# Head loads of an attention stage moved to SyncE's queue in 32-row pieces, and S5 outputs loaded some blocks before their use

## The chip, the cores and the metric

The kernel runs on one core of one Trainium2 chip. The metric is the device time of one execution in microseconds (us), given as the median of three runs. Each engine (PE = TensorE, DVE = VectorE, ACT = ScalarE, POOL = GpSimd) works through its own queue of instructions in order. SP (SyncE) issues most of the DMAs, also in order; a DMA issued there goes through the hardware queue, one issued by POOL through the software queue.

## What is computed

Two layers of a trunk for 1024 latent and 128 context tokens of width 1024. Layer 0 projects the normed tokens to queries, keys, values and S5 inputs, runs differential attention (four heads) and an S5 state-space mixer beside each other, and joins them in one output projection; layer 1 is a pooling mixer; each is followed by a squared-ReLU MLP. The change concerns the attention and the gelu of the S5 output:

```python
q, k, v, u = split_in(h, mix_w_in)          # 4 heads, q and k as two halves of 64
s = einsum('bqhmd,bkhmd->bhmqk', q, k) * scale
p = softmax(s, axis=-1)
w = p[:, :, 0] - lam * p[:, :, 1]           # the two halves m = 0, 1
o = einsum('bhqk,bkhe->bqhe', w, v)         # latents: 1024 + 256 keys, context: its own 128
y = (ys[0] + ys[1]) + d_skip * u            # S5 output, two directions
g = gelu(y)
out = g * sigmoid(g @ w_glu)
```

## The kernel before

Matrix products are made of three passes over operands split into a high and a low part. One helper records every engine instruction, so all stand under line L86; groups are told apart by their tiles.

**Projections.** Twelve steps (four heads, each queries, keys, values), each in three blocks of 384 tokens in the order 2, 0, 1, so 36 blocks `n`. `qk_block` rotates a block, splits it into high and low (tile `zz`) and stores it to DRAM scratch `qS` or `kS`; `v_block` transposes a block (tiles `vz`, `pvt`) and stores it to `vS`. `zz`, `vz` and the cached keys `chl` share three buffers (`rp`), so a block's DVE work can have to wait for the store of an earlier one. All engines follow program order in this stage. The scratch is read back by head, since the score product wants 128 rows of (high, low) by 64 channels where the projection wrote blocks of tokens.

**Head loads.** At `n = 31` the tiles of the heads are opened and the unused halves of four `Kl` tiles are zeroed on POOL. From there `load_head(0)` runs one step per block. For each half m it fills `Q` (128 rows of 1152 floats: the high and low part of the queries), `Kd` (128 rows of 1408: the high keys, twice) and 64 rows of `Kl` (the low keys). One head is 3.34 MB. Its nine DMAs were issued by POOL; the values `Vv` come through SP. Heads 1 to 3 are loaded from block 3 of the head before on, one step per block. There are two buffers of each tile.

**Attention.** 36 blocks (4 heads x 9), then two more turns to empty the pipeline. Block i makes its scores (PE, tiles `SP0`, `SP1`), their maximum (DVE, `nm`), the exponentials (ACT, `e`), the combination (ACT and POOL), the transposes and the product with the values (PE). Only PE keeps program order here; the other engines' queues are ordered by the framework's scheduler when the kernel is built. From block 2 on each block also takes one step of `side_work`: the gelu of four S5 channel tiles (`s5_gelu`: `uf` and `yf` loaded, one buffer each; `yf` = `uf` times the skip factor plus `yf` on DVE; square on ACT; two on POOL; tanh on ACT; product on DVE; split on ACT and DVE), and then the split of the `w_glu` weights (tiles `g`).

**After it** come the output projection, the pooling mixer and the two MLPs, from about 760 us to the end.

**SP's semaphores.** SP's DMAs take eight completion counters in turn, so a DMA waits until the one eight before it has landed.

Of the kernel before, what the change touches and what calls it, by code (L numbers as in the profile page):

```python
# [8 lines left out]
F32 = mybir.dt.float32  # L9
# [63 lines left out]
def build(nc, tc, a, o, probe=None):  # L73
    pinned = set()

    class Engine:
# [5 lines left out]
        def __getattr__(self, op):  # L82
            f = getattr(self.e, op)

            def call(*args, **kw):
                ins = f(*args, **kw)  # L86
                if self.name in pinned:
# [5 lines left out]
    V, A, T, P, S_ = (Engine(n, e) for n, e in (("V", nc.vector), ("A", nc.scalar), ("T", nc.tensor),  # L93
                                                ("P", nc.gpsimd), ("S", nc.sync)))
    dma = S_.dma_start
# [24 lines left out]
    def tt(e, out, x, y, op):  # L120
        return e.tensor_tensor(out, x, y, op=op)

    def stt(e, out, x, s, y, op0, op1):
        e.scalar_tensor_tensor(out, x, s, y, op0=op0, op1=op1)
# [4 lines left out]
    qS = dr([HEADS, 2, 2, 2, 32, NTOK], F32, "qS")  # L129
    kS = dr([HEADS, 2, 2, 2, 32, KEYS + TX], F32, "kS")  # L130
# [746 lines left out]
    def load_head(h):  # L877

        Q = [HB([128, NTOK], F32R, f"Q{m}", bufs=2) for m in range(2)]
        Kd = [HB([128, KEYS + TX], F32R, f"Kd{m}", bufs=2) for m in range(2)]  # L880
        Kl = KL[h % 2]
        Vv = HB([128, 11, 128], F32, "Vv", bufs=2)
        l1 = HB([128, 9], F32, "l1", bufs=2)
        hd[h] = (Q, Kd, Kl, Vv, l1)
        cast = P.dma_start
        cast(Q[0], qS[h, :, :, 0])
        for half in range(2):
            cast(Kd[0][64 * half:64 * half + 64], kS[h, 0, :, 0])
        yield
        cast(Kl[0][0:64], kS[h, 1, :, 0])  # L890
        cast(Q[1][0:64], qS[h, 1, :, 1])
        yield
        cast(Q[1][64:128], qS[h, 0, :, 1])
        cast(Kd[1][0:64], kS[h, 0, :, 1])
        yield
        cast(Kd[1][64:128], kS[h, 0, :, 1])
        cast(Kl[1][64:128], kS[h, 1, :, 1])
        yield
        dma(Vv[:, 0:8], vS[h][:, 0:8])
        dma(Vv[:, 10:11], vS[h][:, 10:11])  # L900
        dma(Vv[:, 8:10], a["cache_v"][h].rearrange("p (t e) -> p t e", t=2))
# [55 lines left out]
    for i in range(12):  # L957
        h, kind = divmod(i, 3)
# [4 lines left out]
        for b in (2, 0, 1):  # L963
            p, last, *c = project(w, b)
            cf = c[0] if c else cf
            before(n)
            if n in KN:
                keys_in(KN[n])
            (qk_block if kind < 2 else v_block)(h, *((kind,) if kind < 2 else ()), b, p, cf, lambda: after(n))
            post(n)  # L970
            if b == 2:
                proj_split(i + 1)
            if n == NS + 9:
                S3.close()
                R.close()
                UR.close()
                HB = Pool("heads", side="right")
                KL = [[HB([128, KEYS + TX], F32R, f"Kl{j}{m}") for m in range(2)] for j in range(2)]
                for kl in KL:
                    for m in range(2):  # L980
                        P.memset(kl[m].bitcast(F32)[64 - 64 * m:128 - 64 * m], 0.0)
                loads = load_head(0)
            if loads:
                next(loads, None)
            n += 1
# [152 lines left out]
    def s5_gelu(i):  # L1138

        uf = AT([128, C8, UC], F32, "uf")  # L1140
        yf = AT([128, C8, UC], F32, "yf")
        dma(uf, uS[128 * i:128 * i + 128])
        for g in range(8):
            dma(yf[16 * g:16 * g + 16], yS[8 * i + g].rearrange("(t x) c -> x t c", t=C8))
        yield
        stt(V, yf, uf, dskip[:, i:i + 1], yf, ALU.mult, ALU.add)
        yield
        A.activation(uf, yf, AF.Square)
        yield
        P.tensor_scalar(uf, uf, 0.044715, 1.0, op0=ALU.mult, op1=ALU.add)  # L1150
        tt(P, uf, uf, yf, ALU.mult)
        yield
        A.activation(uf, uf, AF.Tanh, scale=math.sqrt(2.0 / math.pi))
        yield
        stt(V, uf, uf, 1.0, yf, ALU.add, ALU.mult)
        yield
        segs = []
        for u0, u1, b, c0 in ((0, 48, 0, 0), (48, 96, 1, 0), (96, 128, 2, 0), (CX0, UC, 2, 256)):
            c1 = c0 + 8 * (u1 - u0)
            segs.append((uf[:, :, u0:u1], ga[b][:, i, c0:c1].rearrange("p (c s) -> p s c", s=C8),  # L1160
                         ga[b][:, 4 + i, c0:c1].rearrange("p (c s) -> p s c", s=C8)))
        for u, hv, lv in segs:
            A.activation(hv, u, AF.Copy, scale=0.5)
        yield
        for u, hv, lv in segs:
            stt(V, lv, u, 0.5, hv, ALU.mult, ALU.subtract)

    def side_work():

        for i in range(4):  # L1170
            yield from s5_gelu(i)
        yield
        for j in range(4):
            raw = W([128, 4, 128], F32, "raw", bufs=2)
            dma(raw, a["w_glu"][j])
            if j == 1:
                g1 = W([128, 2, 4, 128], F32R, "g1", tag="raw1")
                hi, lo = g1[:, 0], g1[:, 1]
            else:
                hi, lo = (AT([128, 4, 128], F32R, f"g{j}{q}") for q in (1, 2))  # L1180
            A.activation(hi, raw, AF.Copy)
            tt(V, lo, raw, hi, ALU.subtract)
            wgl.append((hi, lo))
            yield
# [12 lines left out]
    for i, t in enumerate(turns):  # L1197
# [3 lines left out]
        if i < nw:  # L1201
            h, qb = work[i]
# [31 lines left out]
        if i < nw:  # L1234
            if qb == 3 and h + 1 < HEADS:
                loads = load_head(h + 1)
            if loads:
                next(loads, None)
# [72 lines left out]
    x, ah = [], []  # L1311
    blk2 = lambda: (BA([128, KT, BX], F32R, "blk", bufs=3), BB([128, KT, BX], F32R, "blk", bufs=3))
    for b in range(NB):
        t = BB([128, KT, BX], F32R, "blk", bufs=3)
        for k in range(4):
            src = hid([128, BN], F32, ("ph", "pl")[k % 2])
# [415 lines left out]
```

## Time and profile before

| | us |
|---|---|
| median of three runs | 2637.35 (2632.61 to 2638.91) |
| the profiled execution | 2634.18 |
| its span | 2632.4 |
| last projection matmul of PE starts at | 415.23 |
| first score matmul of block 1 starts at | 466.05 |
| attention ends about | 733 |

The page gives busy time and share of the span for each engine. A line of the timeline gives the start, the duration, the engine, the operation with out<-in, and in brackets how long the engine had been idle and who released it. The table of windows gives each engine's busy time in a stretch. The list of DMA issues gives the median time from issue to landing.

### The profile page before, as it was taken

To read this page: it belongs to the slowest core of one execution; us is meant where nothing else is said; L and a number is where in the kernel's file an instruction comes from. 1 tells how busy PE (TensorE), PEld (TensorE's weight loads), DVE (VectorE), ACT (ScalarE), POOL (GpSimd) and SP (SyncE) were. 2 spreads that over 40 slices of the span, in tenths; PEclk is the share of its full clock that TensorE was granted. 3 is DMA by queue.
4 is the path that set the end of the run, shared out by engine and by line. 5 is a ranking of instruction groups with operands and counts; after the bars stand their busy time and mean duration, and the time that the engine had idled before them with its cause. 6 is when DMAs were issued, how large, how long until landed. Compare 5 with 4: busy or idle time off the path is not lost.

```text
span 2632.4 us, 36768 instructions
## 1 busy us (share of the span) xinstructions
PE 2457.9 (93%) x14262; PEld 2299.3 (87%) x14262; DVE 1760.9 (67%) x3530; ACT 909.1 (35%) x1679; POOL 381.0 (14%) x346
## 2 busy tenths in 40 slices
PE   7978893786899999999999999999999999999998
PEld 3866693675799799999999999878999999999996
DVE  7489872797869677777767655756555555565554
ACT  4453372776742522222222221554222222122214
POOL 5465513564400000000000000020000000000002
PEclk8988897898999999999999999999999999999999
DMA  6334689445045122232323111011111111111102
GB/s 236 86 107 122 201 205 162 100 88 70 13 160 192 57 89 80 81 96 65 96 73 96 61 41 33 1 41 49 33 49 49 33 49 41 41 41 41 49 9 72
DMA packets 121662, 210.96 MB, mean 80 GB/s; under 512 B 25744, under 2 KB 82832, under 8 KB 121104
## 3 DMA queue, kind: packets, MB, share of 16 engines
q1 hardware_dynamic: 100240, 189.64, 24.2%
q0 software_dynamic: 19008, 13.44, 3.5%
q10 hardware_dynamic: 2240, 5.54, 0.6%
q8 instruction: 113, 1.85, 0.3%
q14 instruction: 61, 0.50, 0.1%
HBM read 176.95 MB, written 31.56 MB: 79 GB/s over the span
## 4 chain that ended last, share of the span: by engine, by line
PE 71%; DVE 8%; DMA 6%; ACT 2%; issue 2%; POOL 1%; SPq 0%; DVEq 0%; ACTq 0%; POOLq 0%
PE p L86 63%; PE nps L86 2%; PE tp L86 2%; PE SP L86 2%; DVE nm L86 1%; DMA yf<-yS 1%; DMA Kl<-kS 1%; DMA raw<-in_w_dram 1%; DVE vv L86 1%; PE pmm L86 1%; DMA raw<-in_mod_v_dram 1%; DMA Kd<-kS 1%; DVE sc L86 1%; DVE mj L86 1%; ACT e L86 1%
## 5 line engine op out<-in xcount | busy, mean ns | idle before, releaser
L86 PE MATMUL p<-blk,wh 128*128 128x384 f32 (+1 forms) x3072 | 794.9, 339 | 0.3 <-DVE r L86 0.3
L86 DVE SCALAR_TENSOR_TENSOR x<-p,modc,x 128x384 f32<-128x384 f32 (+2 forms) x1056 | 513.7, 513 | 165.6 <-PE p L86 160.7
L86 PEld LDWEIGHTS p<-blk,wh 128*128 128x128 f32 x3072 | 559.1, 189 | 13.3 <-issue 11.9
L86 PE MATMUL p<-blk,wl 128*128 128x384 f32 (+1 forms) x1536 | 521.5, 339 | 0.0
L86 PE MATMUL p<-ph,w2h 128*128 128x384 f32 x1536 | 515.1, 335 | 1.8 <-DVE x L86 1.8
L86 PE MATMUL p<-ph,w2l 128*128 128x384 f32 x1536 | 514.4, 335 | 0.0
L86 PE MATMUL p<-pl,w2h 128*128 128x384 f32 x1536 | 513.7, 334 | 0.0
L86 ACT ACTIVATE r<-r,cf 128x384 f32<-128x384 f32 (+2 forms) x256 | 129.9, 531 | 685.8 <-DVE r L86 685.7
L86 PEld LDWEIGHTS p<-ph,w2h 128*128 128x128 f32 x1536 | 288.3, 188 | 7.1 <-DVE x L86 3.7
L86 PEld LDWEIGHTS p<-blk,wl 128*128 128x128 f32 x1536 | 288.8, 188 | 6.5 <-issue 6.2
L86 PEld LDWEIGHTS p<-ph,w2l 128*128 128x128 f32 x1536 | 288.3, 188 | 2.6 <-issue 2.5
L86 PEld LDWEIGHTS p<-pl,w2h 128*128 128x128 f32 x1536 | 288.3, 188 | 0.8 <-issue 0.6
L86 DVE TENSOR_TENSOR r<-p,y 128x384 f32<-128x384 f32 x192 | 106.2, 553 | 207.7 <-PE p L86 194.6
L86 ACT ACTIVATE wh<-raw 128x1024 fp32r<-128x1024 f32 x80 | 84.8, 1060 | 347.4 <-PE p L86 313.6
L86 DVE SCALAR_TENSOR_TENSOR mj<-raw,cb 128x1024 f32<-128x1024 f32 x128 | 156.0, 1219 | 14.4 <-DMA raw<-in_mod_v_dram 13.1
L86 POOL TENSOR_TENSOR pl<-pl,mx 128x256 f32<-128x256 f32 x18 | 14.8, 827 | 1036.8 <-ACT pl L86 1036.8
L86 ACT ACTIVATE w2h<-raw 128x1024 fp32r<-128x1024 f32 x74 | 77.3, 1057 | 222.4 <-PE p L86 173.1
L86 PE MATMUL pmm<-lo,wh 128*128 128x384 f32 (+1 forms) x384 | 138.2, 360 | 6.4 <-DVE lo L86 6.1
L86 PE MATMUL SP<-Kd,Q 128*128 128x512 f32 (+2 forms) x200 | 81.6, 408 | 65.0 <-ACT e L86 28.6
L86 PE MATMUL pmm<-hi,wh 128*128 128x384 f32 (+1 forms) x384 | 141.4, 369 | 0.8 <-ACT wh L86 0.8
L86 PE MATMUL pmm<-hi,wl 128*128 128x384 f32 (+1 forms) x384 | 137.7, 359 | 1.1 <-DVE wl L86 1.1
L86 POOL TENSOR_TENSOR x<-x,y 128x384 f32<-128x384 f32 x16 | 16.5, 1070 | 818.4 <-DVE y L86 805.3
(287 smaller groups left out, 3627.0 us busy)
## 6 DMA issues: line engine op xcount, KB each, us to landing
raw<-in_w_dram SPq DMA_DIRECT2D x128, 512.0 KB, 3.6
raw<-in_mod_v_dram SPq DMA_DIRECT2D x64, 512.0 KB, 3.5
raw<-in_mod_w_dram SPq DMA_DIRECT2D x25, 512.0 KB, 4.9
raw<-in_w_in_dram SPq DMA_DIRECT2D x16, 512.0 KB, 4.6
Kd<-kS POOLq DMA_DIRECT2D x16, 352.0 KB, 21.9
qS<-zz SPq DMA_DIRECT2D x12, 384.0 KB, 2.7
x<-in_x_dram SPq DMA_DIRECT2D x3, 1536.0 KB, 7.5
out_y_dram<-x SPq DMA_DIRECT2D x24, 192.0 KB, 1.9
```

The lines of the kernel that those rows point to most:

```text
L86: ins = f(*args, **kw)
```

## The change

Two things. `load_head` issues its loads of `Q`, `Kd` and `Kl` on SP, in pieces of 32 rows: 20 DMAs a head where there were nine on POOL (80 and 36 over the four heads), in another order (all of half m = 0 first). `s5_gelu` waits four steps (five for the first tile) after it has issued its loads; the two steps that are saved by putting `yf`'s first operation beside the square, and the last product beside the split, take the count from seven steps a tile to eight, so that side work fills all 38 turns from block 2 on.

```diff
-        cast = P.dma_start
-        cast(Q[0], qS[h, :, :, 0])
-        for half in range(2):
-            cast(Kd[0][64 * half:64 * half + 64], kS[h, 0, :, 0])
-        yield
-        cast(Kl[0][0:64], kS[h, 1, :, 0])
-        cast(Q[1][0:64], qS[h, 1, :, 1])
-        yield
-        cast(Q[1][64:128], qS[h, 0, :, 1])
-        cast(Kd[1][0:64], kS[h, 0, :, 1])
-        yield
-        cast(Kd[1][64:128], kS[h, 0, :, 1])
-        cast(Kl[1][64:128], kS[h, 1, :, 1])
-        yield
+        def rows(t, r0, src):
+
+            for x in range(2):
+                dma(t[r0 + 32 * x:r0 + 32 * x + 32].bitcast(F32), src[x])
+
+        for m in range(2):
+            rows(Q[m], 64 * m, qS[h, 0, :, m])
+            rows(Kd[m], 0, kS[h, 0, :, m])
+            yield
+            rows(Kd[m], 64, kS[h, 0, :, m])
+            rows(Q[m], 64 - 64 * m, qS[h, 1, :, m])
+            rows(Kl[m], 64 * m, kS[h, 1, :, m])
+            yield
...
-        yield
+        for _ in range(4 if i else 5):
+            yield
         stt(V, yf, uf, dskip[:, i:i + 1], yf, ALU.mult, ALU.add)
-        yield
         A.activation(uf, yf, AF.Square)
...
         stt(V, uf, uf, 1.0, yf, ALU.add, ALU.mult)
-        yield
         segs = []
```

**POOL at the start of attention.** `zz` is the rotation of the last key blocks of head 3, `Q`, `Kd` and `Kl` the loads of heads 0 and 1. Before:

```order
L86 MEMSET Kl_3983 64x1408
L86 DMA Q_3988<-qS 128x1x1152
L86 DMA Kd_3990<-kS 64x1x1408 x2
L86 TENSOR_TENSOR zz<-zz,sin 128x384
L86 DMA Q_4307<-qS 128x1x1152
L86 TENSOR_TENSOR zz<-zz 128x384
L86 DMA Kl_3980<-kS 64x1x1408
L86 DMA Q_3989<-qS 64x1x1152 x2
L86 DMA Kd_3991<-kS 64x1x1408 x2
```

After:

```order
L86 MEMSET Kl_3983 64x1408
L86 TENSOR_TENSOR zz<-zz,sin 128x384
L86 TENSOR_TENSOR zz<-zz 128x384
L86 TENSOR_TENSOR e_4208<-e_4208,e_4210 128x1280
L86 TENSOR_TENSOR e_4232<-e_4232,e_4236 128x1280
```

The rotation of the last key block no longer stands between DMA issues.

**SP over the last key and value blocks** (`kS<-zz` and `vS<-vz` are their stores, `chl` the cached keys of head 3). Before:

```order
L86 DMA out_nk_dram<-zz 128x128
L86 DMA chl<-in_cache_k_dram 128x256
L86 DMA kS<-zz 128x2x256
L86 DMA kS<-zz 128x2x128
L86 DMA kS<-zz 128x2x384
L86 DMA raw<-in_w_glu_dram 128x512
L86 DMA kS<-chl 128x2x256
L86 DMA kS<-zz 128x2x384
L86 DMA out_nv_dram<-vz 128x128
```

After:

```order
L86 DMA kS<-chl 128x2x256
L86 DMA Kd_3990<-kS 32x1408 x2
L86 DMA Q_3988<-qS 32x1152 x2
L86 DMA Kl_3980<-kS 32x1408 x2
L86 DMA kS<-zz 128x2x384
L86 DMA Q_3989<-qS 32x1152 x2
L86 DMA Kd_3991<-kS 32x1408 x2
L86 DMA out_nv_dram<-vz 128x128
L86 DMA vS<-vz 128x256
L86 DMA vS<-vz 128x128
L86 DMA Kd_3991<-kS 32x1408 x2
L86 DMA Q_3989<-qS 32x1152 x2
```

Ahead of `kS<-chl` stand five more loads, four of head 0 and one of head 1. So SP now carries the 20 loads of head 0 among the last stores, and a load holds up the store behind it.

**SP around the loads of the last S5 tile** (`cS<-og` are stores of normed heads). Before:

```order
L86 DMA cS<-og 128x384 x2
L86 DMA yf<-yS 16x8x146 x3
L86 DMA uf<-uS 128x1168
L86 DMA cS<-og 128x384
L86 DMA yf<-yS 16x8x146 x5
L86 DMA Vv<-vS 128x1024
```

After:

```order
L86 DMA Kl_3983<-kS 32x1408 x2
L86 DMA cS<-og 128x384
L86 DMA Vv<-vS 128x1024
L86 DMA Vv<-vS 128x128
L86 DMA Vv<-in_cache_v_dram 128x256
L86 DMA cS<-og 128x384
L86 DMA uf<-uS 128x1168
L86 DMA yf<-yS 16x8x146 x8
```

The last S5 tile's loads now follow all loads of head 3, where they ran beside them.

## Rows read from the trace of the kernel before

**Rows 1.** The page: busy us (share) by engine; the chain's lines.

```profile
PE 2457.9 (93%) x14262; PEld 2299.3 (87%) x14262; DVE 1760.9 (67%) x3530; ACT 909.1 (35%) x1679; POOL 381.0 (14%) x346
...
PE p L86 63%; PE nps L86 2%; PE tp L86 2%; PE SP L86 2%; DVE nm L86 1%; DMA yf<-yS 1%; DMA Kl<-kS 1%; DMA raw<-in_w_dram 1%; DVE vv L86 1%; PE pmm L86 1%; DMA raw<-in_mod_v_dram 1%; DMA Kd<-kS 1%; DVE sc L86 1%; DVE mj L86 1%; ACT e L86 1%
```

**Rows 2.** Windows: busy us by engine, PE's granted clock, DMA share, GB/s.

```profile
415.00:466.00 51.00, 6.85 (x22) 4.86 (x21) 4.58 (x8) 5.38 (x10) 6.97 (x11) 0.59 1.20 151
466.00:480.00 14.00, 10.60 (x39) 7.90 (x38) 10.01 (x14) 10.07 (x14) 5.49 (x3) 0.80 0.64 156
...
512.00:583.00 71.00, 57.42 (x381) 50.52 (x380) 66.32 (x116) 52.57 (x90) 43.57 (x26) 0.95 0.42 95
583.00:622.00 39.00, 27.30 (x189) 24.02 (x187) 21.92 (x35) 22.86 (x41) 17.10 (x12) 0.95 1.07 141
622.00:664.00 42.00, 28.56 (x167) 25.41 (x168) 41.41 (x74) 27.16 (x44) 19.96 (x7) 0.80 0.03 9
664.00:720.00 56.00, 48.63 (x351) 43.94 (x351) 46.92 (x95) 43.26 (x74) 23.73 (x9) 1.00 0.03 11
```

**Rows 3.** Timeline of PE, from the last projection to block 1.

```profile
417.60 0.55 PE L86 MATMUL pvt<-ident,vz 128*128 128x128 f32 x3 [2.03 <-ACT vz L86]
440.78 0.80 PE L86 MATMUL SP<-Kd,Q 128*128 128x512 f32 x1 [22.64 <-DVE sgc L86]
...
457.71 0.80 PE L86 MATMUL SP<-Kd,Q 128*128 128x512 f32 x1 [13.79 <-DMA Kd<-kS]
464.20 0.77 PE L86 MATMUL SP<-Kl,Q 128*128 128x512 f32 x1 [5.70 <-DMA Kl<-kS]
...
466.05 0.63 PE L86 MATMUL SP<-Kd,Q 128*128 128x512 f32 x1
```

**Rows 4.** Timeline of DVE, same stretch.

```profile
440.17 0.56 DVE L86 TENSOR_TENSOR vz<-pmm,y 128x384 f32<-128x384 f32 x1 [23.65 <-DMA kS<-zz]
...
445.37 0.68 DVE L86 TENSOR_TENSOR g<-raw,g 128x512 fp32r<-128x512 f32 x1
```

**Rows 5.** DMA, 415 to 465 us: queue's share; issues, KB, median us to landing.

```profile
q0 software_dynamic: 5840, 5.09, 83.6%
...
Kd<-kS POOLq DMA_DIRECT2D x4, 352.0 KB, 32.3
...
kS<-zz SPq DMA_DIRECT2D x1, 384.0 KB, 24.0
```

**Rows 6.** DMA over the whole run and from 380 to 416 us.

```profile
kS<-zz SPq DMA_DIRECT2D x8, 384.0 KB, 2.7
...
DMA packets 8751, 6.68 MB, mean 186 GB/s; under 512 B 1522, under 2 KB 8142, under 8 KB 8750
```

**Rows 7.** Timeline of SP's issues over the last key blocks.

```profile
403.93 2.38 SPq L86 DMA_DIRECT2D kS<-zz  x3
...
409.13 0.36 SPq L86 DMA_DIRECT2D kS<-chl  x1
```

**Rows 8.** S5 loads in a quiet stretch, 495 to 530 us: landing, issue.

```profile
yf<-yS SPq DMA_DIRECT2D x8, 73.0 KB, 3.0
...
499.43 3.17 SPq L86 DMA_DIRECT2D yf<-yS  x7
```

**Rows 9.** Timelines at the last S5 tile; its loads, 586 to 622 us.

```profile
621.63 1.43 DVE L86 SCALAR_TENSOR_TENSOR yf<-uf,pack,yf 128x1168 f32<-128x1168 f32 x1 [14.06 <-DMA yf<-yS]
...
625.97 0.80 PE L86 MATMUL SP<-Kd,Q 128*128 128x512 f32 x1 [12.26 <-ACT e L86]
...
yf<-yS SPq DMA_DIRECT2D x8, 73.0 KB, 17.8
```

**Rows 10.** Tiles Kd and yf: ns min/median/max, first and last start.

```profile
L86 POOL DMA_DIRECT2D Kd<-kS x16: 642/681/714, 410.9 to 597.6; - x16
...
L86 DVE SCALAR_TENSOR_TENSOR yf<-uf,pack,yf x4: 1421/1430/2469, 479.7 to 621.6; 128x1168 f32<-128x1168 f32 x4
```

## The prediction

> **What bounds the kernel now.** I read the page's busy shares and chain of waits first, then the windows over the attention, then the timelines where PE idles, then the DMA lists of those stretches. PE is busy for 93% of the span, POOL for 14% [rows 1]: over the whole run time can only come from PE's gaps. The chain names three DMA lines, the S5 loads and the two key loads, at about 1% each [rows 1], some 26 us each of 2632.4; all lie in the attention, so the argument needs only 415 to 733 us. The MLPs behind it are neither touched nor reordered.
>
> In the first window, 415 to 466 us, PE works 6.85 of 51 us, DVE 4.58 and POOL 6.97, while the DMA engines move 151 GB/s [rows 2]. The timeline of PE divides the gap. It waits 22.64 us for DVE before the first score matmul, then 13.79 for `Kd` and 5.70 for `Kl`; block 1 starts at 466.05, and that is my mark for the end of this phase [rows 3]. The first of these waits is a DMA too, since DVE itself stood 23.65 us for the store `kS<-zz`, whose buffer the last value block needs [rows 4]. That store took 24.0 us to land there [rows 5], 2.7 as the median of the whole run [rows 6]. Beside it the software queue held 83.6% of the DMA engines, and its `Kd` loads took 32.3 us [rows 5]. So one crowd of software loads causes all three waits.
>
> The other gap is at 621.63: DVE waits 14.06 us for the last `yf`, and PE 12.26 [rows 9]. Those loads took 17.8 us, beside the loads of head 3 [rows 9]; in a quiet stretch they took 3.0 [rows 8]. Outside the gaps PE and DVE bound by turns: DVE is busy for 66.32 of 71 us from 512 and 41.41 of 42 from 622, PE 48.63 of 56 from 664 [rows 2].
>
> **Loads of head 0.** Removed: nine software loads, and with them the crowd in front of the last key store. Added: 20 hardware loads on SP, and their place ahead of the last stores. No row shows a 32-row load of 147 to 180 KB, so I bound it from both sides by when block 1 can start.
>
> *Early end.* If only issuing costs, one issue takes 3.17 / 7 = 0.45 us [rows 8]. `kS<-chl` goes out at 409.13 [rows 7], and five loads stand before it now: 409.13 + 5 x 0.45 = 411.4. Behind it stand 16 loads of head 0 and four stores, 20 x 0.45 = 9.0 us. With the landing of 3.0 [rows 8] and the 1.85 from `Kl`'s arrival to block 1 (464.20 to 466.05 [rows 3]) that makes 425: a gain of 41.
>
> *Late end.* SP has eight counters, so loads go in rounds of eight. At the 17.8 us of a crowded S5 load [rows 9] the 16 loads behind 411.4 are two rounds, some 34 us: block 1 at about 445, a gain of 21.
>
> *Taken.* Head 0 is 3.34 MB. At the 186 GB/s that mostly hardware traffic made from 380 to 416 us [rows 6] it takes 18 us: 411.4 + 18 + 1.85 = 431. I take 430, nearer to the early end, because the stretch just before moved data at this rate with stores landing in 2.7 us [rows 6]: **-36**, bounds -41 to -21. What is late next is the issue order on SP: the last value stores stand behind loads, but nobody needs their data before block 1's product.
>
> In the crowd the engines moved 151 GB/s with a share of 1.20 of their time [rows 2]; were the number of rows the limit, smaller pieces would not help. A rule that speaks against the pieces stands in the Trainium skill, SBUF — State Buffer, section "Door 1: The DMA port swizzle (why [64,N] ≈ [32,N])": 32 partitions reach only 8 of 16 ports, measured there at 189 GB/s. No run here shows it yet; by it the loads, if one ran at a time, would take an estimated 17.7 us, against 18 by the row, so the sum would stay.
>
> **Loads of the S5 tiles.** `uf` and `yf` are now asked for four blocks before use, and their neighbours are hardware loads. From 466 to 720 us [rows 2] 35 blocks run, with the 14 us stall among them: (254 - 14) / 35 = 6.9 us a block, so they have some 27 us, more than the 17.8 of the crowded case [rows 9]. The 14.06 us of DVE goes; DVE is what is busy right behind it (41.41 of 42 us [rows 2]), so its idle time is the measure and not PE's 12.26: **-14**, bounds -10 to -16 (the upper one with a `yf` operation of 1.43 [rows 9] out of the way, too). The loads of the other three tiles were not waited for, and gain nothing.
>
> **Clock.** From 622 to 664 us the granted clock averages 0.80 [rows 2], PE's two levels being 1.2 and 2.4 GHz: 40% of 42, or some 17 us, at the lower one, right after the 12 us gap. If the gap goes, that stretch may go too; but DVE is full there, so PE's slower pace is mostly hidden: **-2**, bounds 0 to -4. The same fall at 466 to 480 (0.80 [rows 2]) stays, since PE still idles before it.
>
> **POOL.** 36 issues of about 0.68 us [rows 10] leave it, 24.5 us, and so do the waits between them, behind which stood the rotation of the last key block and some additions in `combine`. POOL works 43.57 of 71 us in the fullest window [rows 2], so only what stood behind a wait can count: **-2**, bounds 0 to -4.
>
> **Side work moved.** The first tile's `yf` operation (2.47 us, the longest of four [rows 10]) ran while DVE waited for loads, and so did two splits of `w_glu` at 0.68 [rows 4]: 2.47 + 1.36 = 3.8 us now stand in blocks where DVE is the limit. The side work ends five turns later, with the last tile's two long products beside the norm of head 2. **+4**; bounds 0, where they fall into PE-bound blocks, and +10, where the last tile's products cost in full as well. Two operations in one step instead of two cost nothing: the scheduler orders DVE and ACT anyway.
>
> **Sum.** -36 - 14 - 2 - 2 + 4 = -50. Against the profiled execution 2634.18 - 50 = 2584; the median shown is 3.2 above that execution, so 2637.35 - 50 = **2587**. With every term at its better bound it is 2572 (-41 - 16 - 4 - 4 + 0); with block 1 at 438, halfway to the late end, -12 for the S5 wait and nothing from clock and POOL it is 2601 (-28 - 12 + 4). So the forecast's own range is 2572 to 2600.
>
> **Rivals.**
>
> *Rounds of eight.* Hardware loads crowd each other as they did the S5 loads beside the software queue [rows 9]; head 0 takes the late end. -21 - 14 - 2 - 2 + 4 = -35 at its best; a late `Vv` or a late S5 load takes up to 14 more: 2602 to 2616, about 2606. For it speaks the single queue with all loads and stores; against it the quiet 3.0 us [rows 8].
>
> *No gain at the start.* The crowd was the data itself: a share of 1.20 at 151 GB/s [rows 2], and 3.34 MB take as long through any queue. Then only the S5 wait goes: 2637 - 14 - 2 + 1 = 2622. Against it: 186 GB/s [rows 6].
>
> *One after another, slower than before.* If a 32-row load occupies the queue for t until it has landed, head 0's 20 loads and the two stores among them last from 404 to 404 + 22 t, where block 1 started at 466. Heads 2 and 3 are asked for six blocks ahead, 6 x 6.9 = 41 us, and need 20 t, and 5 us for values: each stalls 20 t - 36 (head 1's loads follow head 0's at once and have nine blocks). With t at the 3.0 us of a quiet landing [rows 8]: +4 at the start, 2 x 24 at the heads, -14 for the rest, +38: 2675. It decides from t = 2.4 on: (404 + 53 - 466) + 2 x 12 - 14 is about zero. Against it: seven S5 loads were issued in 3.17 us and each landed in 3.0 [rows 8], so they overlapped.
>
> The Trainium skill, same page, section "The DMA setup-cost knee (why "@ 1 MiB" ≠ asymptote)", gives a fixed cost of about 2 us for each DMA on top of its bytes: an estimated 2.4 us for one of these loads. Paid one after another, that stands just at the point of decision, an estimated 2638; the trace's overlapped loads speak against paying it so.
>
> *The S5 wait stays.* The change doesn't do what it says if the scheduler or SP's order holds the last `uf` back: its loads now stand behind all 20 of head 3. -36 - 2 + 4 - 2: 2601.
>
> **Chances.** Forecast 0.70 (2572 to 2600); rounds of eight 0.17 (to 2616); no gain at the start 0.06; one after another 0.04; S5 wait stays 0.03. The forecast alone falls short of 8 in 10, so the range takes in the rounds of eight: 2572 to 2616. About 0.3%, 8 us, can be told from no change. Only the serial loads end above 2645, and half of the no-gain case within 8 us of before: faster 0.93, same 0.03, slower 0.04.
>
> **What would show it.** In the profile after: block 1's first score matmul near 430, and at the latest 445; the last `vz` operation on DVE no longer waiting for `kS<-zz`; that store's landing below 10 us; head loads landing in 3 to 8 us; no DVE wait for `yf` above 2 us; the clock near full from 600 to 660. The prediction is wrong if 32-row loads take over 2 us apiece one after another, if the last key store waits on SP behind loads as long as it waited in the crowd, or if the blocks at 512 to 583 us become longer because DVE has the moved work as well.

## The result, and the profile after

The changed kernel takes 2594.76 us (median of four runs, 2594.05 to 2597.87), the kernel before 2638.13 beside it (2632.61 to 2643.42). The ratio is 0.9838 with a 95% interval of 0.9816 to 0.9860: faster by 43.4 us, where 50 were forecast. The profiled execution took 2594.47 us (span 2592.7), 39.7 less than the one before.

On the page, PE's share rises with the shorter span and its busy time hardly changes (2461.2 us where 2457.9 stood, [rows 1]); `Kd` and `yf` are gone from the chain, and two small DMA lines of head loads are left.

```profile
PE 2461.2 (95%) x14262; PEld 2303.9 (89%) x14262; DVE 1772.0 (68%) x3530; ACT 908.5 (35%) x1679; POOL 360.3 (14%) x310
...
PE p L86 66%; PE nps L86 2%; DVE nm L86 2%; DVE vv L86 2%; PE pmm L86 1%; PE tp L86 1%; PE SP L86 1%; ACT e L86 1%; DMA Q<-qS 1%; DMA raw<-in_w_dram 1%; DVE sc L86 1%; DMA raw<-in_mod_v_dram 1%; DVE sq L86 0%; DVE wl L86 0%; DMA Kl<-kS 0%
```

The start of the attention on PE's timeline, which answers to [rows 3]: the three waits of 22.64, 13.79 and 5.70 us are now 2.89, 2.48 and 0.60, and block 1 starts at 430.37 where 466.05 stood.

```profile
421.52 0.50 PE L86 MATMUL SP<-Kd,Q 128*128 128x512 f32 x1 [2.89 <-DVE sgc L86]
...
427.16 0.77 PE L86 MATMUL SP<-Kd,Q 128*128 128x512 f32 x1 [2.48 <-DMA Kl<-kS]
428.53 0.77 PE L86 MATMUL SP<-Kl,Q 128*128 128x512 f32 x1 [0.60 <-DMA Kl<-kS]
...
430.37 0.63 PE L86 MATMUL SP<-Kd,Q 128*128 128x512 f32 x1
```

DVE's timeline has the wait for the last key store at 5.73 us instead of 23.65 [rows 4], and none before the last S5 tile's `yf`, where 14.06 stood [rows 9]:

```profile
420.91 0.56 DVE L86 TENSOR_TENSOR vz<-pmm,y 128x384 f32<-128x384 f32 x1 [5.73 <-DMA kS<-zz]
...
636.62 1.43 DVE L86 SCALAR_TENSOR_TENSOR yf<-uf,pack,yf 128x1168 f32<-128x1168 f32 x1
```

The DMA list from 415 to 465 us (queue's packets, MB and share; issues with KB and median us to landing) answers to [rows 5]. `Kd`, in pieces of half the size, lands in 5.2 us where it took 32.3, the store in 5.1 where it took 24.0:

```profile
q1 hardware_dynamic: 4778, 9.34, 74.4%
...
Kd<-kS SPq DMA_DIRECT2D x12, 176.0 KB, 5.2
...
kS<-zz SPq DMA_DIRECT2D x1, 384.0 KB, 5.1
```

To see where the rest went, the attention is cut at the first maximum (DVE, `nm`) of blocks 1, 9, 18, 27 and 35, so roughly by head. Before (windows with the columns of [rows 2]):

```profile
468.40:521.70 53.30, 43.48 (x259) 37.64 (x260) 42.54 (x65) 42.88 (x69) 32.78 (x17) 0.90 0.37 96
521.70:586.90 65.20, 54.17 (x353) 47.51 (x352) 61.34 (x104) 49.37 (x82) 38.83 (x23) 0.95 0.39 87
586.90:665.40 78.50, 53.61 (x339) 47.58 (x340) 60.13 (x108) 49.31 (x84) 33.61 (x18) 0.87 0.52 69
665.40:715.40 50.00, 43.55 (x312) 39.45 (x312) 43.00 (x87) 39.50 (x65) 20.39 (x7) 1.00 0.03 9
```

After:

```profile
432.80:482.00 49.20, 39.63 (x260) 34.12 (x261) 43.78 (x64) 42.56 (x68) 28.98 (x11) 1.00 0.38 88
482.00:548.30 66.30, 52.10 (x341) 46.30 (x340) 56.91 (x104) 46.61 (x79) 29.60 (x11) 0.92 0.37 83
548.30:615.50 67.20, 54.69 (x354) 48.88 (x353) 59.81 (x103) 47.23 (x80) 29.70 (x11) 0.90 0.37 88
615.50:675.10 59.60, 48.85 (x321) 43.65 (x319) 53.72 (x87) 43.91 (x71) 26.38 (x9) 0.92 0.15 40
```

Start -35.6, head 0 -4.1, head 1 +1.1, head 2 -11.3, head 3 +9.6, and from block 35 to the gate's first product 6.6 us where 4.8 stood, +1.8. The rest of the program is 1.2 us shorter. So the start gave 35.6 of 39.7 us, and what head 2 gained by its wait head 3 gave back: DVE works 53.72 us there instead of 43.00.

### The profile page after: what moved, and what is told of

Same layout as the page of the kernel before. It is cut to its first block, busy times and chain, and to the rows that moved or that the text cites. A ratio compares the mean times of both kernels' runs of the same rounds, so it can differ in the third digit from the quotient of the medians.

```text
span 2592.7 us, 36810 instructions
## 1 busy us (share of the span) xinstructions
PE 2461.2 (95%) x14262; PEld 2303.9 (89%) x14262; DVE 1772.0 (68%) x3530; ACT 908.5 (35%) x1679; POOL 360.3 (14%) x310
## 4 chain that ended last, share of the span: by engine, by line
PE 73%; DVE 9%; DMA 4%; ACT 2%; issue 1%; SPq 0%; POOL 0%; DVEq 0%; ACTq 0%
PE p L86 66%; PE nps L86 2%; DVE nm L86 2%; DVE vv L86 2%; PE pmm L86 1%; PE tp L86 1%; PE SP L86 1%; ACT e L86 1%; DMA Q<-qS 1%; DMA raw<-in_w_dram 1%; DVE sc L86 1%; DMA raw<-in_mod_v_dram 1%; DVE sq L86 0%; DVE wl L86 0%; DMA Kl<-kS 0%
## 5 line engine op out<-in xcount | busy, mean ns | idle before, releaser
L86 DVE TENSOR_TENSOR s<-r 128x384 f32<-128x384 f32 x192 | 106.5, 555 | 39.5 <-ACT r L86 39.3
```

## The experiments

**Which of the two edits?** Each was tried alone. For the loads alone:

```diff
-        for _ in range(4 if i else 5):
-            yield
+        yield
         stt(V, yf, uf, dskip[:, i:i + 1], yf, ALU.mult, ALU.add)
+        yield
         A.activation(uf, yf, AF.Square)
...
         stt(V, uf, uf, 1.0, yf, ALU.add, ALU.mult)
+        yield
```

> The changed loads of Q, Kd and Kl, with the S5 steps as they were before. The changed kernel measured 2594.8; its profile puts block 1 at 430.4 (-35.7 us against before), and gives nearly all of the rest back in the last head, whose eight blocks take 59.5 us against 50.0. Theory A, the moved side work costs those 9.5 us and the S5 wait goes with the software loads alone: block 1 at 430, no DVE wait for yf above 3 us, last head near 50 us, 2585 (2582 to 2589). Rival, the early S5 loads are needed, since the last yf loads now stand behind head 3's loads in one queue: a wait of 5 to 14 us for yf stays, 2593 to 2600.

Measured 2594.01 us (2591.82 to 2596.76), ratio 0.9846 (0.9832 to 0.9860): the same as with both edits. That is in the rival's range, but for a reason that neither theory named. No wait for `yf` stood out (the largest was 0.61 us), so half of theory A held: the early S5 loads are not what removed the 14 us. But the last head took 67.4 us, with one block of 21.5. DVE's timeline there has the last tile's chain in a row:

```profile
615.64 1.44 DVE L86 SCALAR_TENSOR_TENSOR yf<-uf,pack,yf 128x1168 f32<-128x1168 f32 x1 [0.61 <-DMA raw<-in_w_glu_dram]
...
623.50 1.38 DVE L86 SCALAR_TENSOR_TENSOR uf<-uf,yf 128x1168 f32<-128x1168 f32 x1 [5.96 <-ACT uf L86]
625.84 2.44 DVE L86 SCALAR_TENSOR_TENSOR blk<-uf,blk 128x384 fp32r<-128x384 f32 x4 [0.96 <-ACT blk L86]
```

From the first to the last of them DVE waits for square, POOL and tanh with almost nothing between, and PE waits for a copy of `wt` that stands behind:

```profile
630.32 0.90 PE L86 MATMUL tp<-ident,of 128*128 128x128 f32 x3 [13.97 <-DVE wt L86]
```

The scheduler had put the chain so. For the S5 steps alone, `load_head` is as before:

> The S5 loads and steps as changed, with the head loads on POOL's software queue in large pieces as before. Both theories: block 1 at 466. Theory A (the S5 wait goes, some 11 us, and the last head becomes 9.5 us longer): 2632 to 2638, no difference from before that can be told. Rival, as the prediction had it (-14 for the wait, +4 for moved work): 2626 to 2630.

Measured 2635.95 us (12 executions), ratio 1.0010 (0.9996 to 1.0025): no change, as theory A had it, but not by its sum. Block 1 is at 463.5, the last head is 50.4 us, and the wait is still there, only for the third tile, in spite of four blocks of lead:

```profile
588.80 1.44 DVE L86 SCALAR_TENSOR_TENSOR yf<-uf,pack,yf 128x1168 f32<-128x1168 f32 x1 [11.05 <-DMA yf<-yS]
```

The third tile's `uf` and its last `yf` load went out only at 570.43 and 570.86 us, behind a store of a normed head in SP's queue:

```profile
570.00 0.34 SPq L86 DMA_DIRECT2D cS<-og  x1
570.43 0.38 SPq L86 DMA_DIRECT2D uf<-uS  x1
570.86 0.43 SPq L86 DMA_DIRECT2D yf<-yS  x1
```

So the head loads carry the whole gain, and beside the old ones the S5 shift only moves a wait.

**Queue or pieces?** The load edit changes both. First the queue without the pieces:

```diff
-            for x in range(2):
-                dma(t[r0 + 32 * x:r0 + 32 * x + 32].bitcast(F32), src[x])
+            dma(t[r0:r0 + 64].bitcast(F32), src)
```

> As changed, but each pair of 32-row loads is one load of 64 rows on the same queue (10 loads a head). Theory 'queue', it is the hardware queue that counts: landings near 5 us, block 1 within 3 us of 430, 2592 to 2598. Theory 'pieces', the source of such a load is two separate runs of 32 rows, and it lands much later than a 32-row load: landings above 10 us, block 1 after 450, head starts late as well, above 2615. The Trainium skill, DMA: Bandwidth & Descriptors, in its section on why a DMA increments its semaphore by 16, says that the number of DMA engines a load is spread over divides the sizes of the slowest dimensions, which is 2 for this shape and 16 for 32 rows; an estimate by that page is an eighth of the rate, and a time above 2640.

Measured 2697.42 us (2695.28 to 2699.56), ratio 1.0241 (1.0220 to 1.0262): slower than before by 62.7 us, with block 1 at 483.1. PE's waits at the start:

```profile
447.35 0.80 PE L86 MATMUL SP<-Kd,Q 128*128 128x512 f32 x1 [19.33 <-DVE sgc L86]
...
473.74 0.77 PE L86 MATMUL SP<-Kd,Q 128*128 128x512 f32 x1 [23.12 <-DMA Q<-qS]
481.25 0.76 PE L86 MATMUL SP<-Kl,Q 128*128 128x512 f32 x1 [6.75 <-DMA Kl<-kS]
```

The first block of head 1 takes 26.2 us, with waits of PE of 13.35 us for `Q` and 6.93 for `Kl`. The first of head 2 takes 26.2 too, but there PE waits only 6.73 us for `Kl`, and DVE 18.17 for a `yf`; a block of 27.7 us late in head 2 has DVE's wait of 20.16 us for the last `yf`. Head 3 does not begin late. For loads of this shape the hardware queue alone is a loss. Then the pieces without the queue, the inner `dma` being `P.dma_start`:

> As changed, but the 32-row loads go through POOL's software queue. Theory 'queue': the software queue crowds the DMA engines whatever the piece, kS<-zz lands after 15 us or more, block 1 after 450, 2620 to 2650, the more since POOL now has 80 issues of some 0.68 us (54 us). Theory 'pieces': landings near 5 us and block 1 near 430, 2595 to 2600.

Measured 2594.71 us (two executions), ratio 0.9851 (0.9827 to 0.9875). Once the pieces are small, the kernel takes the same time with either queue. The start is not the same: block 1 is at 437.0, and SP's transfers are slow beside these loads, so that DVE waits 15.65 us for the first tile's `yf`. The tile's rows (ns of one issue; us to landing, min/median/max):

```profile
L86 POOL DMA_DIRECT2D Kd<-kS x32: 492/492/573, 411.7 to 608.5; - x32
...
DMA to landing us min/median/max: 2.8/3.4/9.9
```

Half the bytes, but 3.4 us instead of the 21.9 that such a load took before. With the S5 steps as before as well, only the size of the pieces and their order differ from the kernel before:

> Only the size of the pieces is changed: 32-row loads on POOL's software queue, S5 steps as before. The run with both changes on the software queue gave 2594.7, with block 1 at 437 and a first block of 25.0 us, since DVE waited 15.65 us for the first tile's yf. Theory A, the pieces are the whole effect, and the S5 steps neither gain nor lose: 2590 to 2598. Theory B, the early S5 steps put that wait there, and the loads on another queue than SP don't need them: block 1 near 437, first block about 13, last head near 50 us, 2580 to 2588.

Measured 2595.27 us (2592.95 to 2600.79), ratio 0.9852 (0.9829 to 0.9876): theory A in the time. Theory B's reason fell too: DVE still waits 15.4 us for the first tile's `yf`, with the old steps, so the shift had not put that wait there.

**Rows or runs?** A load of 64 rows reads two separate runs of 32 rows, since the half m lies inside x in the scratch. With m outside x the 64 rows are one run:

```diff
+    def put(d, c0, c1, src):
+        for x in range(2):
+            for m in range(2):
+                p = 64 * x + 32 * m
+                dma(d[:, m, x, :, c0:c1].rearrange("i r c -> r i c"), src[p:p + 32])
...
-            rows(Q[m], 64 * m, qS[h, 0, :, m])
+            rows(Q[m], 64 * m, qS[h, 0, m])
...
-                dma(t[r0 + 32 * x:r0 + 32 * x + 32].bitcast(F32), src[x])
+            dma(t[r0:r0 + 64].bitcast(F32), src.rearrange("x r c -> (x r) c"))
```

> As the run with 64-row loads on the hardware queue (2697.4, block 1 at 483.1), but with the scratch laid out so that the 64 rows of a load are one run of rows instead of two; the stores are made in four pieces of 32 rows instead of one. Theory 'two runs', the load was slow for its source's shape: loads land within 8 us, block 1 by 435, 2593 to 2604. Theory 'rows', 64 rows are too many for one load: landings above 10 us, block 1 after 450, above 2640.

Measured 2592.68 us (two executions), ratio 0.9840 (0.9808 to 0.9871): 'two runs', against 2697.4 for the same number of loads of the same size on the same queue. Its landings are 6.3 us for 352 KB in the median (the longest, 11.0, is above the 8 that the theory gave):

```profile
L86 SPq DMA_DIRECT2D Kd<-kS x16: 444/594/596, 417.0 to 566.7; - x16
DMA to landing us min/median/max: 4.2/6.3/11.0
```

Block 1 missed its mark (443.6, not 435): the projections, where the four stores a block in place of one are the only edit, end 12.4 us later (the last matmul starts at 430.4 instead of 418.0); the attention made that up (below). The pair separates runs from rows on SP's queue. On the software queue they were not separated: there only 64 rows in two runs and 32 rows in one were tried.

**Is the start all?** Head 0 in pieces on SP, heads 1 to 3 and the S5 steps as before:

> Head 0 alone is loaded in 32-row pieces on SP; heads 1 to 3 and the S5 steps are as before. Theory A, the gain is the start alone (block 1 at 430 instead of 466), while the S5 wait of 11 to 14 us stays and the last head is short: 2598 to 2604. Rival, head 1's large loads now crowd head 0's and the last stores: block 1 after 440, above 2608.

Measured 2622.66 us (2620.82 to 2623.41), ratio 0.9952 (0.9934 to 0.9970): the rival. Block 1 is at 458.4, and pieces that landed in 5.2 us in the changed kernel take 15.7 there, beside the nine large loads of head 1 that POOL issues from 409 to 431 us (the list is from 415 to 460):

```profile
q1 hardware_dynamic: 2503, 4.66, 62.4%
q0 software_dynamic: 4080, 3.13, 47.5%
...
Kd<-kS POOLq DMA_DIRECT2D x2, 352.0 KB, 36.4
...
Kd<-kS SPq DMA_DIRECT2D x4, 176.0 KB, 15.7
```

So a large load hurts the small ones that run beside it, and a single queue has a merit: it puts head 1 behind head 0. The next pair shows it with small pieces alone. Heads 1 to 3 go through POOL's queue, head 0 through SP's, with the new S5 steps and with the old ones:

> As changed, but heads 1 to 3 are loaded in 32-row pieces through POOL's software queue; head 0 stays on SP. Theory A, SP's one queue costs something in the changed kernel (S5 loads and the stores of normed heads stand behind 60 head loads), and the pieces alone keep the DMA engines free: block 1 near 431, attention from block 1 on 243 to 249 us instead of 251.3, 2586 to 2592. Rival, the attention's time does not depend on the queue of the loads: 2593 to 2598.

> The same with the S5 steps as before. The run with all pieces on the software queue and these steps took 243.1 us from block 1 on, though PE stood 12.1 us in it for the first tile's yf, and its block 1 was at 436.7. Theory A, the yf of the first tile lands early when SP carries only head 0: block 1 near 431, attention 231 to 240 us, 2575 to 2584. Rival, the scheduler's order brings another stall instead, as in the runs before: 2590 to 2598.

Measured 2598.10 us (ratio 0.9856, 0.9837 to 0.9876) and 2593.32 us (0.9838, 0.9820 to 0.9856): the rivals' times, but not their reasons. POOL is free early and issues the loads of head 1 from 411 and 409 us on; block 1 is late, at 443.0 and 441.3. In the second of them the two queues hold 60.5% and 37.0% of the DMA engines from 405 to 441 us, and `Kd` of head 0 lands in 10.0 us, of head 1 in 8.4:

```profile
Kd<-kS POOLq DMA_DIRECT2D x8, 176.0 KB, 8.4
...
Kd<-kS SPq DMA_DIRECT2D x6, 176.0 KB, 10.0
```

From block 1 on the attention was indeed shorter, 243.5 and 238.1 us against 251.3, and the late start took it back.

**What sets the attention?** Three steps of lead for the S5 tiles instead of four:

> As changed, with three steps between an S5 tile's loads and its first operation instead of four (four instead of five for the first): seven steps a tile, as before, so that the side work ends some four blocks earlier. Theory A, the last head's 59.5 us come from where the last tile's steps fall: last head 50 to 55 us, 2585 to 2591. Rival, DVE's work costs the same wherever it falls, or a DMA is then waited for: 2593 to 2598.

Measured 2597.20 us (2595.98 to 2600.45), ratio 0.9859 (0.9838 to 0.9879): the rival's time, but not by its reason. The last head has a block of 21.5 us again, as with the loads alone, and takes 67.4 us. It is the place of the S5 chain in DVE's queue that differs, and the scheduler chose that. So DVE's program order was kept in the attention, with the changed steps and with the old ones:

```diff
-PINA = "T"
+PINA = "TV"
```

> As changed, with DVE as well as PE in program order during the attention. Theory 'order': where the S5 steps and norms fall in DVE's queue is the scheduler's choice, and the blocks of 8 to 11 us, four in each head of the changed kernel, come from it: in program order the attention changes by more than 5 us either way from 251.3, and each head's slow blocks move. Rival 'work': DVE's work sets the time whatever its order: 249 to 254 us from block 1 on, 2592 to 2598.

> The changed loads with the S5 steps as before, and DVE in program order during the attention, so that the S5 steps stand where they are written. The run in program order with the changed steps took 2589.4, with the last head's eight blocks at 57.9 us and no wait for yf. Theory A, with loads that land in 5 us a tile needs no four blocks of lead, and an earlier end of the side work relieves the last head: no yf wait above 3 us, last head 50 to 53 us, 2581 to 2586. Rival, one block of lead is too short, since the S5 loads now stand behind head loads on SP: DVE waits 5 us or more for yf and holds its queue, 2589 to 2600.

Measured 2589.40 us with the changed steps (2587.24 to 2592.96; ratio 0.9827, 0.9805 to 0.9850) and 2601.83 with the old ones (2599.85 to 2604.47; 0.9864, 0.9839 to 0.9889). The first is the shortest of all kernels here, but its interval overlaps that of the changed kernel, so it is not shown to be faster. Its attention is 4 us shorter (247.1): under the 5 that theory 'order' asked for, and below the range of 'work'. Between the two medians the shift is worth 12.4 us, by the ratios some 10, and their intervals touch. The second is its rival's case in the wait, though slower than its range. DVE's waits in it (the transfer named is a neighbour in SP's queue; the tile's own last `yf` load landed 0.2 to 0.4 us before DVE went on):

```profile
DVE yf L86 <- DMA cS<-og: 6.0, 1, 6.0
...
DVE yf L86 <- DMA Q<-qS: 3.7, 1, 3.7
```

Together they are 9.7 us. In program order one block of lead is too short, although the loads land in 4.5 us: `uf` has one buffer, and SP holds its load, and all that stands behind it, until DVE has split the tile before (`blk`). Before the second of these waits (from 520 us on):

```profile
SPq L86 <- DVE blk L86: 38.5, 1, 38.5
...
542.33 0.34 SPq L86 DMA_DIRECT2D uf<-uS  x1
542.76 4.30 SPq L86 DMA_DIRECT2D yf<-yS  x8
```

DVE came to that tile's `yf` at 544.4 us, before its last load was issued, and went on at 550.36. In the scheduler's order the shift was worth nothing (2594.76 and 2594.01).

## Why the prediction was right, and where it was not

The time lies in the range and the sign is right; the largest term was hit for a reason that was half wrong, and two others missed by about as much as the sum did.

- **Loads of head 0: -36, measured -35.7** (block 1 at 430.37, forecast 430). That one crowd of software loads caused all three waits held: all three fell together. That the software queue made the crowd fell. The step "nine software loads removed, 20 hardware loads added" should have read: large loads whose source is in several runs, removed. The same queue with small pieces gives the same time, the other queue with large ones 2697.4. I had put the pieces aside as a size to be bounded, and the queue as the cause. That the figure was met within 1 us was luck in part. I took 18 us at the 186 GB/s of [rows 6]; the stretch from 415 us to block 1 moved 285 GB/s, and what set the time was SP's issuing, the path of the early end:

```profile
412.43 0.36 SPq L86 DMA_DIRECT2D kS<-chl  x1
...
423.48 0.77 SPq L86 DMA_DIRECT2D Kl<-kS  x2
```

`kS<-chl` went out 1.0 us later than I had it (411.4), the 20 issues behind it took 11.8 us instead of 9.0, and from there it was 4.3 us, instead of 3.0, to PE's product with the last `Kl` at 428.53: some 5 us on the early end's 425.

- **The S5 wait: -14, measured -11.3 in head 2.** The wait went, but not for the shift: with the loads alone it went too, and with the shift alone 11.05 us stayed. The rival *the S5 wait stays* was true of that edit by itself.
- **Side work moved: +4, measured about +11** (+9.6 in the last head, +1.8 behind it). This is the mis-sized term, and its bound of +10 was the nearer one. The last tile's work on DVE, two products and four splits, falls in the last head: 53.72 us of DVE against 43.00. Where it falls earlier on a free queue (software pieces, old steps) that head takes 52.6 us; where it falls earlier but in a row, 67.4. So the term is the place of the chain in DVE's queue, not only its length.
- **Clock: -2, no gain seen.** From 622 to 664 us the granted clock is 0.92 instead of 0.80 [rows 2], but in the last head it fell from 1.00 to 0.92. The forecast of a clock near full from 600 to 660 was wrong: it was 0.86.
- **POOL: -2, not seen.** With 80 issues of 0.49 us on POOL the time is the same, so these issues cost nothing either way.
- **The rivals.** *Rounds of eight*: the rounds are there, but cheap. In the changed kernel a load of head 0 goes out as the transfer eight before it lands (`Kd` at 420.80, the last key store having landed at 420.78); they land in 3.1 to 6.2 us (`Kd`) and not in 17.8, and from 398 to 432 us SP's waits for DMAs add up to 4.2 us, the longest 0.7. *No gain at the start*: the crowd was not the data. *One after another, slower than before*: it did not occur with 32 rows, which land in 5 us and overlap; with 64 rows in two runs much the same did, at 2697: from 487.25 us, when SP issued the next of head 1's loads, it took 67 us until PE had the last `Kl` (554.68). The start and head 1 were late for it; in heads 2 and 3, where the rival had the stalls, the waits were mostly for `yf`. The case that was given 0.04 lay one line of the diff away.

Left open: why the attention from block 1 on took between 235.9 us (the other layout of the scratch) and 263.4 us (program order with the old steps) in the kernels without two-run loads, with the same arithmetic. A late start went with a short attention (443.6 with 235.9, 441.3 with 238.1, 430.4 with 251.3), and all of them but one (in order with the old steps) reach the gate between 674 and 687 us. Part of it is DVE's order, as the pair in program order shows; that DVE uses a late start for S5 work is likely but was not measured by itself.

## What to carry to other kernels

Before a slow load is moved to another queue, look at the shape of its source: large loads that each read two runs of rows can be several times slower than twice as many loads of one run each (53 against 285 GB/s here). On the hardware queue the two runs are shown to be the reason; on the software queue only that smaller pieces cure it, and that the large ones slow down what runs beside them. Whether an early load pays is decided in the queue of the engine that uses it; where a scheduler orders that queue, a shift of the steps may only move the stall. And loads with a deadline belong ahead of the rest in one queue: a second queue that was free too early took the DMA engines from them, and the stage began 11 to 13 us later (here the attention made that up).

## What the runs showed of the hardware

The page counts DMA packets by queue, and packets under 512 B. Before:

```profile
DMA packets 121662, 210.96 MB, mean 80 GB/s; under 512 B 25744, under 2 KB 82832, under 8 KB 121104
...
q1 hardware_dynamic: 100240, 189.64, 24.2%
q0 software_dynamic: 19008, 13.44, 3.5%
```

After:

```profile
DMA packets 106494, 210.90 MB, mean 81 GB/s; under 512 B 10576, under 2 KB 67664, under 8 KB 105936
...
q1 hardware_dynamic: 104080, 203.01, 26.5%
```

64-row loads on the hardware queue, and 32-row loads on the software queue:

```profile
q1 hardware_dynamic: 102880, 203.00, 24.4%
```

```profile
q0 software_dynamic: 3840, 13.37, 2.0%
```

64-row loads on the hardware queue with the other layout of the scratch, where their source is one run:

```profile
q1 hardware_dynamic: 104976, 203.01, 26.5%
```

The four heads have 2560 rows to load. 80 loads of 32 rows add 3840 packets on either queue: 2560 + 80 x 16. 40 loads of 64 rows in two runs add 102880 - 100240 = 2640 = 2560 + 40 x 2. With the other layout, 40 loads of 64 rows in one run and 96 more stores add 104976 - 100240 = 4736 = 2560 + (40 + 96) x 16. So a two-run load leaves two short packets where a one-run load leaves sixteen, with 32 rows or with 64. By the Trainium skill, DMA: Bandwidth & Descriptors, section "Why a DMA increments its semaphore by 16 and not by 1", each DMA engine that takes part in a load ends its share with a write to the load's semaphore, and their number is the largest up to 16 that divides the sizes of the slowest dimensions on both sides: two engines for two runs. If the short packets are these writes, the counts agree with it, and so does the share of the DMA engines where head loads run almost alone. The windows of that run, with the columns of [rows 2]:

```profile
432.00:442.00 10.00, 0.00 (x0) 0.00 (x0) 0.00 (x0) 0.00 (x0) 0.00 (x0) 0.51 0.13 53
...
520.00:530.00 10.00, 8.39 (x62) 7.23 (x61) 9.89 (x17) 10.00 (x19) 6.11 (x2) 1.00 0.13 53
```

A share of 0.13 is two engines of 16, the eighth that the expectation named, and 53 GB/s is all that these loads got, against the 285 of the changed kernel's start.

The software queue fails in another way: it holds 83.6% of the DMA engines [rows 5], not an eighth. Its 36 large loads left 19008 packets for the same 2560 rows, so 16448 are short. Three loads of 64 rows stand alone in the kernel before, from 475 to 500 us:

```profile
q0 software_dynamic: 1584, 1.09, 20.6%
```

They have 192 rows, so each leaves 464 short packets; of the 16448 that leaves 400 for each of the four loads of 128 rows, which read four runs, where a 32-row load leaves 16. The short packets' own time does not make the crowd: from 415 to 465 us the trace has 4861 of them, of 4 bytes and 9 ns each in the median, 103 us in all, beside 565 us of 979 data packets, of the 800 us that 16 engines have. A data packet takes 522 ns there in the median. Why it takes so long, and whether the short packets have a part in that, stays open.
